# A hybrid decoder step in fp32 on one core: first branch's product between the Gated DeltaNet's steps, a hand-written TensorE order at the change of stages, residual in whole rows

## The chip, the cores and the metric

One Trainium2 chip, one core. The metric is the device time of one launch in microseconds (us). The kernel before takes 2064.81 us, the median of three runs (2064.51 to 2070.0).

## What is computed

One step of a one-layer decoder trunk on 1032 tokens (1024 of a prompt, 8 new ones of a sample), width 1024, all in fp32. Cut to what matters here (RWKV-7 gives `o_a`, the Gated DeltaNet `o_b`, both 512 wide):

```
proj = rmsnorm(h) @ w_in
o_a = rwkv7(proj);  o_b = gated_delta_chunked(conv(proj))
gate_a, gate_b = sigmoid(...)
mix = gate_a * (o_a @ w_branch_a) + gate_b * (o_b @ w_branch_b)
h = h + mix @ w_out
u2 = rmsnorm(h)
h = h + (silu(u2 @ w_ffn_gate) * (u2 @ w_ffn_up)) @ w_ffn_down
h = h + sigmoid(rmsnorm(h) @ w_ple_gate) * (pe @ w_ple_proj);  y = rmsnorm(h)
# gated_delta_chunked: tinv = (I + L)^-1 for each chunk and head, then
v_new = u_c - w_c @ S;  o = qg_c @ S + qk_c @ v_new
S = S * gl_c + kd_c.T @ v_new            # eight chunks (0 to 7), in turn
```

## The kernel before

Tokens lie along the free axis, channels on the 128 partitions: 1032 columns in 3 blocks of 344, or 4 of 258. Each fp32 product is three TensorE products (`mm`, L75), high half by high, high by low, low by high, which add up in a PSUM tile named `acc`. `weights` loads a tile of weights `ws` on SyncE's queue (SP), ScalarE (ACT) copies the high half `wh` (L186), GpSimd (POOL) subtracts for the low half `wl` (L187). `split` does the same with data on ACT and VectorE (DVE) (L246, L247).

The first half runs under `order` (L112). A stream of the 46 tiles of the input product is cut into single `acc` products, and tasks (RWKV features, chains of small products, the DeltaNet's inverses, steps, preparations, posts) come back when a clock of `mm`'s making has moved on: `yield 64.0` means "after 64 us of products". So TensorE's order is fixed when the program is built. `inverses` (L1065) inverts 32 x 32 triangles on DVE, ends that part with three transposes to AN and tm (L1090 to L1092), yields 64.0, then issues thin 32 x 32 products (`f<-AN,LT`, `f<-tm,LT`, `f<-LT,W`) four at a time between stream products, has GpSimd clear the tile W (L1128), and issues 64 x 64 products. GpSimd also carries a chain of updates for the sample's state (`St`, `st`, L1190 to L1198).

`steps`, `preps` and `posts` are the DeltaNet's chunks: a step is `x<-S,kc`, `o<-S,q`, `x<-X,LT`, `x<-x,Kd`, `o<-x,M` in turn, a post transposes (`f<-cs,ob`) and normalises to `ob_d` in DRAM. When the tasks are done, `o_a` and `o_b` are loaded in whole rows to U and split, then branch a is a plain `dense` (L1388 to L1390: 288 products of 344 columns, evacuated by DVE into U), then branch b (384 of 258), whose evacuation is a gate load, DVE (L1416), GpSimd's add of U (L1417) and a split to `mx`.

From there a priority scheduler sets the order. `mixer_out(t)` for the two halves t of the tokens adds the input x, stores the residual to `h_d`, and gathers squares; `square` then sends the sum through a product with ones (`f<-c`), `inv_rms` (DVE, with `f<-nre`) and an ACT copy to R. `mixes(t)` multiplies by the norm (L1452) and makes the Strassen operands `xh`, `xl` (L1461 to L1464). The per-layer product `ph` (144 products of 344 columns) follows `mixer_out(1)`; then come the FFN's gate and up products in Strassen form (the first gate product does half t=0 before t=1) and, per group of hidden tiles, the down product, which loads and stores the residual in blocks (L1619, L1626).

Of the kernel before, what the change touches and what calls it, by code (L numbers as in the profile page):

```python
# [9 lines left out]
F32 = mybir.dt.float32  # L10
# [16 lines left out]
KT = 8  # L27
# [31 lines left out]
def hybrid(ctx, tc, a, o):  # L59
# [102 lines left out]
    def scratch(name, shape):  # L162
        return o[name] if name in o else dram.tile(shape, F32, name=name)
# [38 lines left out]
    def cols(b):  # L202
        return b if isinstance(b, slice) else slice(b * BW, (b + 1) * BW)
# [83 lines left out]
    def stream(jobs):  # L287
# [45 lines left out]
        for n, ti in enumerate(jobs[3:], 3):  # L333
            if n == 3:
                nxt = fetch(ti)
            w = nxt
            tc.cur_priority -= LATER
            if n + 1 < len(jobs):
                nxt = fetch(jobs[n + 1])
            tc.cur_priority += LATER  # L340
            for b in range(NBLK):
                yield from product(ti, *w, b)

    def kvr(f):
        return [4 + f, 8 + f, f]
# [720 lines left out]
    def inverses():  # L1066
# [78 lines left out]
    def gdn_sample():  # L1145
# [207 lines left out]
    tasks += [Task(-2 * LATER, steps()), Task(U_, preps()), Task(-LATER, posts())]  # L1353
    order(tasks, dense_in, list(tasks))
    gstk.close()
    psg.close()


    ustk, astk, bstk = ExitStack(), ExitStack(), ExitStack()
    hU = pool(ustk, "hU", 1, "right")  # L1360
    U = [hU.tile([P, TOK], F32, name=f"U{m}") for m in range(KT)]

    def pair(pl_, name, n):
        return [[pl_.tile([P, TOK], F32R, name=f"{name}{q}{k}") for k in range(n)] for q in "hl"]

    obh, obl = pair(pool(bstk, "brb", 1, "right"), "ob", HB)
    oah, oal = pair(pool(astk, "bra", 1, "right"), "oa", 4)
    for src, hi, lo, u0 in ((oa_d, oah, oal, 0), (ob_d, obh, obl, 4)):
        for f in range(4):
            SP.dma_start(U[u0 + f], src[f])  # L1370
        for b in range(NBLK):
            for f in range(4):
                split(U[u0 + f][:, cols(b)], None, hi[f][:, cols(b)], lo[f][:, cols(b)])
    order([], dense_in, [])
    xstk.close()
    tstk = ExitStack()
    tmp = pool(tstk, "tmp", 2)
    banks += 2 * [ctx.enter_context(tc.tile_pool(name="psn", bufs=4, space=PSUM))]

    depth = [3]  # L1380

    def tile(tag, n=BW):
        return tmp.tile([P, n], F32, tag=tag, name=tag, bufs=depth[0] if tag == "a" else 2)

    for m in range(KT):
        def evac(b, ps, m=m):
            g = tile("a")
            SP.dma_start(g, gate_d[m, :, cols(b)])  # L1388
            stt(U[m][:, cols(b)], g, 1.0, ps, ADD, MULT)
        dense(a["wa"][m], 4, oah, oal, evac)  # L1390
    astk.close()
    QW, HW = TOK // 4, TOK // 2
    QB = [slice(i * QW, i * QW + QW) for i in range(4)]
    pas, m1stk, m0stk, xastk, pbs, sstk = (ExitStack() for _ in range(6))
    hq = [pool(pas, "h0", 1), None]
    H, RN, mx = [None, None], [None, None], [None, None]

    def part_of_h(t):
        H[t] = [hq[t].tile([P, HW], F32, name=f"H{t}{m}") for m in range(KT)]
        RN[t] = hq[t].tile([P, HW], F32, name=f"R{t}")  # L1400

    part_of_h(0)
    mx[1], mx[0] = pool(m1stk, "mx1", 1), pool(m0stk, "mx0", 1)
# [6 lines left out]

    for m in range(KT):
        def evac(c, ps, m=m):
            g = tile("a")[:, :QW]
            SP.dma_start(g, gate_d[KT + m, :, c])
            y = tile("c")[:, :QW]
# [3 lines left out]
        dense(a["wb"][m], HB, obh, obl, evac, QB)  # L1419
    bstk.close()  # L1420
    ustk.close()

    def square(m, c, src, ac, R, pl_, newd, last=False):

        if m == 0:
            act(ac, src, AF.Square)
            return
        d = newd(width(c))
        act(d, src, AF.Square)
        if m < KT - 1:  # L1430
            gtt(ac, ac, d, ADD)
            return
        ps = ft([P, width(c)])
        if last:
            mm(ps, ones, ac, start=True, stop=False)
        else:
            tt(d, d, ac, ADD)
        mm(ps, ones, d, start=not last, stop=True)
        inv_rms(R, ps, pl_, ft)
# [5 lines left out]
    def mixes(pl_, t):  # L1445


        hi, lo = ([pl_.tile([P, 4, QW], F32R, tag=f"x{q}{i}", name=f"x{q}{t}{i}") for i in range(7)] for q in "hl")
        tc.cur_priority += (2 - t) * LATER
        y = []  # L1450
        for m in range(KT):
            stt(H[t][m], H[t][m], vc("nffn", m), RN[t], MULT, MULT)  # L1452
            y.append([H[t][m][:, :QW], H[t][m][:, QW:]])
        for i in SIX:
            for k in range(4):
                (y11, y12), (y21, y22) = y[k], y[k + 4]
# [8 lines left out]
        tc.cur_priority -= (2 - t) * LATER  # L1465
        return hi, lo

    def mixer_out(t):
        sq = [hq[t].tile([P, QW], F32, tag=f"sq{i}", name="sq") for i in range(2)]
        for m in range(KT):  # L1470
            def evac(c, ps, m=m):
                i = c.start // QW % 2
                x = tile("a")[:, :QW]
# [15 lines left out]
    for k in range(2):
        for b in range(NBLK):  # L1490
            y = tile("a")
            SP.dma_start(y, a["peT"][k, :, cols(b)])
            split(y, None, ph[k][:, cols(b)], pl[k][:, cols(b)])
    mixer_out(1)
    m1stk.close()
    pas.close()
    tstk.close()
    hstk = ExitStack()
    xb = pool(ctx, "xm1", 1)
    XM[1] = mixes(xb, 1)  # L1500
    sgp = pool(hstk, "sg", 1)
    for m in range(KT):
        po = sgp.tile([P, TOK], F32, tag=f"sg{m % 2}", name="po")

        def evac(b, ps, m=m, po=po):
            act(po[:, cols(b)], ps, AF.Copy)
            SP.dma_start(pp_d[m, :, cols(b)], po[:, cols(b)])
        dense(a["wpp"][m], 2, ph, pl, evac)
    sg = [sgp.tile([P, TOK], F32, tag=f"sg{i}", name=f"sg{i}") for i in range(2)]

    def strassen(src, j, evac, apart=False):
# [64 lines left out]
        for x in second:  # L1578
            part(*x)

    f0 = 0
    for n in (2, 4, 4, 4, 4, 4):
        for j in range(0, n, 2):
# [11 lines left out]
            if f0 + j == 0:  # L1595
                pbs.close()
                hp = pool(hstk, "hid")
                hh, hl = pair(hp, "hid", 4)
                tmp = pool(hstk, "tf", 2)
                depth[0] = 6  # L1600
            strassen(a["wu"], f0 + j, up)
        final = f0 + n == NF
        if final:
# [9 lines left out]
            R = ux.tile([P, TOK], F32, name="R")  # L1613
            idr = diagonal(ux, EW)
        for m in range(KT):
            def evac(b, ps, m=m):
                c = cols(b)
# [119 lines left out]
```

## Time and profile before

| | us |
|---|---|
| median of the runs | 2064.81 |
| the profiled execution | 2082.16 |
| its span | 2080.3 |
| TensorE busy | 1953.9 (94%) |
| DVE busy | 1326.4 (64%) |
| ACT busy | 847.1 (41%) |
| GpSimd busy | 995.5 (48%) |
| mean granted clock of TensorE | 0.962 of full |

Busy shares are means over stages with different limits. A clock column of 1.00 is 2.4 GHz, 0.50 is 1.2 GHz. An idle time in brackets behind an instruction is its engine's wait, with what ended it.

### The profile page before, as it was taken

How to read it: one execution, taken by the hardware profiler on the slowest of the kernel's cores; microseconds unless marked ns; L12 is line 12 of the kernel's file. 1: busy time of each engine (PE TensorE's matmuls, PEld its weight loads, DVE VectorE, ACT ScalarE, POOL GpSimd, SP SyncE). 2: the span in 40 equal slices, each digit the busy share in tenths (PEclk: the TensorE clock that was granted, in tenths of full speed). 3: DMA queues.
4: the chain of work that ended last, by engine and by line, in shares of the span. 5: the costliest groups of instructions: out<-in, count | busy, mean ns of one | idle time of the engine just before them, and what ended most of it. 6: DMA issues, size and time to landing. Idle time of an engine off the chain costs nothing.

```text
span 2080.3 us, 40640 instructions
## 1 busy us (share of the span) xinstructions
PE 1953.9 (94%) x14904; PEld 1826.7 (88%) x14904; DVE 1326.4 (64%) x3300; ACT 847.1 (41%) x2069; POOL 995.5 (48%) x1084
## 2 busy tenths in 40 slices
PE   7988999898999999999799988799999999999996
PEld 7987788776788879899799978799999999999995
DVE  7378676897998369536553787464643635446767
ACT  3333354555554342147423454241423414235532
POOL 1455453666573246641056553553645546364722
PEclk9998999999999999689899999999999999999998
DMA  4442332342343436444446542625244262433312
GB/s 149 142 131 77 109 106 69 111 133 81 93 136 112 147 90 172 143 123 134 166 138 178 159 148 80 188 62 174 77 123 138 72 187 69 135 110 114 109 49 92
DMA packets 218496, 250.89 MB, mean 121 GB/s; under 512 B 48408, under 2 KB 176296, under 8 KB 218296
## 3 DMA queue, kind: packets, MB, share of 16 engines
q1 hardware_dynamic: 218296, 248.30, 39.3%
q8 instruction: 117, 1.92, 0.4%
q14 instruction: 83, 0.68, 0.1%
HBM read 170.82 MB, written 77.40 MB: 119 GB/s over the span
## 4 chain that ended last, share of the span: by engine, by line
PE 55%; DVE 14%; issue 4%; ACT 3%; DMA 2%; POOL 1%; SPq 0%; DVEq 0%; ACTq 0%; POOLq 0%
PE acc L75 48%; PE f L75 2%; PE c L75 1%; DVE xl L1464 1%; PE f L79 1%; PE x L75 1%; DVE ms L1461 1%; DVE inv L731 1%; DVE H L1452 1%; PE zp L75 1%; ACT uxh L249 1%; DVE tm L1085 1%; DVE GM L694 1%; DVE U L1620 0%; PE o L75 0%
## 5 line engine op out<-in xcount | busy, mean ns | idle before, releaser
L75 PE MATMUL acc<-xh,wh 128*128 128x258 f32 (+2 forms) x2360 | 734.1, 312 | 17.5 <-ACT wh L186 8.8
L75 PE MATMUL acc<-xl,wh 128*128 128x258 f32 (+2 forms) x2360 | 737.2, 313 | 13.5 <-DVE xl L1464 7.0
L75 PE MATMUL acc<-xh,wl 128*128 128x258 f32 (+1 forms) x2336 | 726.8, 312 | 0.0
L187 POOL TENSOR_TENSOR wl<-ws,wh 128x512 fp32r<-128x512 f32 (+1 forms) x256 | 336.1, 1315 | 455.9 <-ACT wh L186 452.5
L75 PEld LDWEIGHTS acc<-xh,wh 128*128 128x128 f32 (+1 forms) x2360 | 454.6, 193 | 25.5 <-ACT wh L186 9.0
L75 PEld LDWEIGHTS acc<-xl,wh 128*128 128x128 f32 (+1 forms) x2360 | 456.2, 193 | 23.4 <-DVE xl L1464 8.2
L75 PEld LDWEIGHTS acc<-xh,wl 128*128 128x128 f32 x2336 | 451.6, 193 | 5.5
L186 ACT ACTIVATE wh<-ws 128x512 fp32r<-128x512 f32 (+1 forms) x256 | 157.2, 615 | 254.2 <-PE acc L75 202.6
L187 POOL TENSOR_TENSOR wl<-s,wh 128x512 fp32r<-128x512 f32 x110 | 143.5, 1306 | 148.9 <-ACT wh L186 143.5
L75 PE MATMUL acc<-hidl,wh 128*128 128x344 f32 x528 | 169.4, 321 | 0.0
L75 PE MATMUL acc<-hidh,wh 128*128 128x344 f32 x528 | 166.9, 320 | 2.6 <-DVE a L1620 1.9
L75 PE MATMUL acc<-hidh,wl 128*128 128x344 f32 x528 | 168.8, 320 | 0.0
L1620 DVE TENSOR_TENSOR a<-a,acc 128x344 f32<-128x344 f32 x120 | 60.9, 512 | 125.5 <-PE acc L75 108.7
L186 ACT ACTIVATE wh<-s 128x512 fp32r<-128x512 f32 x110 | 69.3, 631 | 150.1 <-PE acc L75 103.9
L1570 POOL TENSOR_TENSOR s<-ws 128x512 f32<-128x512 f32 x66 | 87.7, 1330 | 53.0 <-DMA ws<-in_wg 44.6
L75 PEld LDWEIGHTS acc<-hidh,wh 128*128 128x128 f32 x528 | 98.8, 188 | 4.1 <-DVE a L1620 1.6
L75 PEld LDWEIGHTS acc<-hidl,wh 128*128 128x128 f32 x528 | 99.3, 188 | 0.3 <-DVE hidl L247 0.3
L75 PEld LDWEIGHTS acc<-hidh,wl 128*128 128x128 f32 x528 | 99.3, 188 | 0.0
L454 POOL TENSOR_TENSOR cy<-cy,cu 128x344 f32<-128x344 f32 x72 | 70.4, 978 | 48.8 <-ACT cu L453 47.4
L75 PE MATMUL acc<-mxh,wh 128*128 128x258 f32 x256 | 72.7, 284 | 0.0
L75 PE MATMUL acc<-mxl,wh 128*128 128x258 f32 x256 | 72.6, 284 | 0.0
L75 PE MATMUL acc<-mxh,wl 128*128 128x258 f32 x256 | 72.2, 282 | 0.0
(469 smaller groups left out, 4018.8 us busy)
## 6 DMA issues: line engine op xcount, KB each, us to landing
ws<-in_win SPq DMA_DIRECT2D x92, 256.0 KB, 3.3
a<-h_d SPq DMA_DIRECT2D x120, 172.0 KB, 2.7
h_d<-a SPq DMA_DIRECT2D x120, 172.0 KB, 2.7
pa_d<-gs SPq DMA_DIRECT2D x90, 172.0 KB, 2.3
ws<-in_wg SPq DMA_DIRECT2D x44, 256.0 KB, 3.2
ws<-in_wu SPq DMA_DIRECT2D x44, 256.0 KB, 3.0
ws<-in_wd SPq DMA_DIRECT2D x40, 256.0 KB, 2.7
gate_d<-gs SPq DMA_DIRECT2D x48, 172.0 KB, 2.5
```

The costliest lines, as they stand in the source:

```text
L75: last[0] = TE.matmul(out, w, x, start=start, stop=stop).ins
L79: last[0] = TE.transpose(out, x, ident).ins
L186: act(h, s, AF.Copy)
L187: (eng or gtt)(l, s, h.bitcast(F32), SUB)
L249: act(hi, src, AF.Copy, scale=gain)
L454: gtt(y, y, u, ADD)
L694: stt(GM[:, 2 * (c + j) + h], ps[h][:, j], cvf[:, cg, h:h + 1], rwmask, MULT, MULT)
L731: tt(w, XA[:, :ns, :nj], LB[:, i:i + 1, :nj].to_broadcast([P, ns, nj]), MULT)
L1085: tt(tm4[:, :i, :i], XT4[:, :i, :i], LB4[:, i:i + 1, :i].to_broadcast([P, i, i]), MULT)
L1452: stt(H[t][m], H[t][m], vc("nffn", m), RN[t], MULT, MULT)
L1570: e(s, A_[p], A_[q], op)
L1620: tt(y, y, ps, ADD)
```

## The change

1. `inverses` yields 68.0 in place of 64.0.
2. Branch a becomes a task, `branch_a`, whose products are taken between the DeltaNet's steps; it loads `o_a` in blocks into the input tiles `xh`, `xl` (0 to 3), and its results go to a new DRAM tensor `u_d`. `branch_b` loads and splits `o_b` as the posts 2, 5 and 7 end. U and its whole-row loads go; branch b's evacuation loads `u_d`.
3. From `mixer_out(0)` to the per-layer product TensorE's order is as written. The sums of squares of a half go in one `sums_of_squares` (one ones-product per quarter, one `rsq` for both), the norm stays in PSUM, and L1452's 8 multiplications of 516 columns become 16 of 258.
4. The down product's residual moves in whole rows of 1032 columns.

```diff
-        yield 64.0
+        yield 68.0
...
+    def branch(src, f, b, k):
+        y = gsp.tile([P, BW], F32, tag="cy", name="ab")
+        SP.dma_start(y, src[f, :, cols(b)])
+        split(y, None, xh[k][:, cols(b)], xl[k][:, cols(b)])
+    def branch_a():
+        yield "win", "branches"
...
+        nxt = weights(a["wa"][0], 4)
+        yield 6.0
+        for m in range(KT):
+            wh, wl = nxt
+            for b in range(NBLK):
...
+                SP.dma_start(g, gate_d[m, :, c])
...
+                    yield 0.0
+                stt(g, g, 1.0, ps, ADD, MULT)
+                SP.dma_start(u_d[m, :, c], g)
...
+    def branch_b():
+        for b, m in enumerate((2, 5, 7)):
+            yield "win", ("post", m), "sampled"
+            for h in range(HB):
+                branch(ob_d, h, b, 4 + h)
...
-            g = tile("a")[:, :QW]
+            g, u = tile("a"), tile("u")
             SP.dma_start(g, gate_d[KT + m, :, c])
+            SP.dma_start(u, u_d[m, :, c])
...
-            gtt(y, y, U[m][:, c], ADD)
+            gtt(y, y, u, ADD)
...
+        for g in range(2):
+            ps = ft([P, QW])
+            mm(ps, ones, sq[g], start=True, stop=True)
+            tt(e[:, g], ps, idr, MULT)
...
-            stt(H[t][m], H[t][m], vc("nffn", m), RN[t], MULT, MULT)
+            for g in range(2):
+                stt(y[m][g], R[g], vc("nffn", m), y[m][g], MULT, MULT)
...
+    with tc.manual_schedule(engines={mybir.EngineType.PE}):
...
+        mixer_out(1, (0,), sq1)
+        e = sums_of_squares(0, sq)
+        mixer_out(1, (1,), sq1)
+        XM[0] = mixes(xa, 0, e)
...
+        for m in range(KT):
+            per_layer(m)
+            if m == 1:
+                e = sums_of_squares(1, sq1)
+            if m == 3:
+                XM[1] = mixes(xb, 1, e)
...
-                y = U[m][:, c] if final else tile("a")
-                SP.dma_start(y, h_d[m, :, c])
+            y = U[m] if final else rows.tile([P, TOK], F32, tag="row", name="row")
+            SP.dma_start(y, h_d[m])
...
+            if not final:
+                SP.dma_start(h_d[m], y)
```

The tile pool of `u` holds two buffers, that of `row` three.

TensorE at the end of the DeltaNet's steps, before: the last stream products, then two steps with nothing between, the last posts, and branch a.

```order
L75 MATMUL x<-x,Kd 128x128 x4
L75 MATMUL o<-x,M 128x128 x4
L79 MATMUL f<-cs,v 128x128 x4
L75 MATMUL f<-q,kc 128x128 x4
L75 MATMUL x<-S,kc 128x128 x4
L75 MATMUL o<-S,q 128x128 x4
L79 MATMUL f<-cs,q 128x128 x4
L75 MATMUL x<-X,LT 128x128 x4
L75 MATMUL x<-x,Kd 128x128 x4
L75 MATMUL o<-x,M 128x128 x4
L79 MATMUL f<-cs,ob 128x128 x8
L75 MATMUL acc<-oah_11765,wh 128x344 x3
```

The same place with the change: branch a's products stand in the last step (`xh_102` to `xh_105` are the input tiles that now hold `o_a`).

```order
L75 MATMUL x<-X,LT 128x128 x2
L75 MATMUL acc<-xh_104,wh 128x344
L75 MATMUL acc<-xl_112,wh 128x344
L75 MATMUL acc<-xh_104,wl 128x344
L75 MATMUL acc<-xh_105,wh 128x344
L75 MATMUL acc<-xl_113,wh 128x344
L75 MATMUL acc<-xh_105,wl 128x344
L75 MATMUL x<-x,Kd 128x128 x4
L75 MATMUL o<-x,M 128x128 x4
```

What moved: 3 to 9 products of branch a lie between the small ones of the last steps, and one step stays without.

DVE behind `mixer_out(1)`, before: the sum of the first Strassen operands (`s<-ws`, of two weight tiles) near the end of the first of two norm chains.

```order
L241 SCALAR_TENSOR_TENSOR nrr<-nrr 128x3
L242 SCALAR_TENSOR_TENSOR nrr<-nrr 128x3
L240 TENSOR_TENSOR nrr<-nrr 128x3
L241 SCALAR_TENSOR_TENSOR nrr<-nrr 128x3
L1570 TENSOR_TENSOR s<-ws 128x512
L242 SCALAR_TENSOR_TENSOR nrr<-nrr 128x3
L282 TENSOR_SCALAR nre<-idr,nrr 128x128 x2
L282 TENSOR_SCALAR nre<-idr,nrr 128x2
L273 TENSOR_TENSOR nre<-f,idr 128x258
```

The same place with the change.

```order
L1501 TENSOR_TENSOR sq_13744<-sq_13744,c 128x258
L1612 TENSOR_TENSOR s<-ws 128x512
L1452 TENSOR_TENSOR e_14621<-f,idr_14541 128x258 x2
L1453 TENSOR_REDUCE r_14620<-e_14621 128x2
L1454 TENSOR_REDUCE r_14620<-e_14621 128x1
```

What moved: `s<-ws` stands ahead of the one chain that is left. On TensorE the ones-product of t=1 came behind 15 `ph` products; with the change the two stand behind 36, and the two products `f<-e` 36 behind those.

SP at the first down product, before: the next gate's last weights behind the residual's blocks (all 24 loads and 21 of 24 stores stand ahead).

```order
L1626 DMA h_d<-a 128x344
L1619 DMA a<-h_d 128x344
L1626 DMA h_d<-a 128x344
L1520 DMA ws<-in_wg 128x512
L1626 DMA h_d<-a 128x344 x2
L1520 DMA ws<-in_wu 128x512
L1626 DMA h_d<-a 128x344
```

The same with the change: the weights go ahead of most rows.

```order
L1562 DMA ws<-in_wg 128x512
L1691 DMA h_d<-row 128x1032
L1562 DMA ws<-in_wg 128x512
L1691 DMA h_d<-row 128x1032
L1562 DMA ws<-in_wu 128x512
L1679 DMA row<-h_d 128x1032
```

What moved: the fourth load of `in_wg` stands behind three loaded rows and one stored row, and no longer behind 24 loads and 21 stores.

## Rows read from the trace of the kernel before

**Rows 1.** The page, busy time of each engine
```profile
PE 1953.9 (94%) x14904; PEld 1826.7 (88%) x14904; DVE 1326.4 (64%) x3300; ACT 847.1 (41%) x2069; POOL 995.5 (48%) x1084
```

**Rows 2.** Busy time by stretch (us, then busy and count of each engine, clock, DMA)
```profile
852.00:894.00 42.00, 42.00 (x386) 32.88 (x386) 9.77 (x28) 8.52 (x15) 28.71 (x39) 0.50 0.49 142
...
962.00:988.00 26.00, 23.49 (x191) 22.91 (x190) 17.48 (x68) 22.08 (x93) 3.21 (x5) 1.00 0.49 137
988.00:1012.00 24.00, 13.01 (x89) 10.71 (x90) 12.74 (x50) 11.78 (x51) 0.00 (x0) 0.79 0.34 104
1012.00:1016.00 4.00, 4.00 (x16) 4.00 (x17) 4.00 (x10) 3.91 (x11) 0.00 (x0) 0.58 1.02 417
...
1060.00:1105.00 45.00, 45.00 (x379) 45.00 (x377) 30.60 (x61) 16.48 (x38) 32.98 (x38) 1.00 0.48 135
...
1345.00:1800.00 455.00, 455.00 (x3496) 455.00 (x3495) 238.21 (x479) 162.06 (x345) 228.87 (x177) 1.00 0.37 113
```

**Rows 3.** Timeline of PE where the thin products begin
```profile
849.12 0.32 PE L75 MATMUL acc<-xl,wh 128*128 128x344 f32 x1
849.37 0.24 PE L75 MATMUL f<-AN,LT 32*32 32x32 f32 x2
851.28 0.21 PE L75 MATMUL f<-tm,LT 32*32 32x32 f32 x1 [1.67 <-DVE tm L1092]
```

**Rows 4.** Timeline of POOL in the thin stretch
```profile
873.57 0.61 POOL L1195 TENSOR_TENSOR st<-kr,sw 128x256 f32<-128x256 f32 x1 [0.67 <-DVE sw L1194]
...
878.16 0.61 POOL L1195 TENSOR_TENSOR st<-kr,sw 128x256 f32<-128x256 f32 x1 [0.99 <-DVE sw L1194]
...
892.11 1.80 POOL L1128 MEMSET W<- 64x2048 f32 x1 [0.83 <-PE f L75]
```

**Rows 5.** PE's waits, 975 to 1016 (total, times, longest), and tile U's splits (ns)
```profile
PE f L79 <- ACT ob L1342: 6.4, 3, 2.9
PE acc L75 <- ACT oah L246: 6.0, 1, 6.0
...
L246 ACT ACTIVATE oah<-U x12: 473/475/497, 1011.3 to 1015.9; 128x344 fp32r<-128x344 f32 x12
```

**Rows 6.** Groups of branch b's evacuation, 1062 to 1104 (busy, mean ns)
```profile
L1417 POOL TENSOR_TENSOR c<-c,U 128x258 f32<-128x258 f32 x29 | 21.7, 749 | 11.1 <-DVE c L1416 8.4 <-ACT wh L186 2.3
...
L1416 DVE SCALAR_TENSOR_TENSOR c<-a,acc 128x258 f32<-128x258 f32 x29 | 12.3, 424 | 6.1 <-PE acc L75 4.2
```

**Rows 7.** DMA issues: branch b, whole span, 990 to 1020 (KB, us to landing)
```profile
a<-gate_d SPq DMA_DIRECT2D x29, 129.0 KB, 2.2
...
a<-h_d SPq DMA_DIRECT2D x120, 172.0 KB, 2.7
...
U<-oa_d SPq DMA_DIRECT2D x4, 516.0 KB, 5.3
```

**Rows 8.** Timeline of DVE from the end of `mixer_out(1)`
```profile
1217.74 0.69 DVE L1570 TENSOR_TENSOR s<-ws 128x512 f32<-128x512 f32 x1 [2.77 <-DMA ws<-in_wg]
...
1221.50 0.43 DVE L273 TENSOR_TENSOR nre<-f,idr 128x258 f32<-128x258 f32 x1 [1.23 <-PE f L75]
...
1230.38 9.59 DVE L1452 SCALAR_TENSOR_TENSOR H<-H,vec,R 128x516 f32<-128x516 f32 x8 [1.87 <-ACT R L285]
...
1271.28 0.42 DVE L1464 TENSOR_TENSOR xl<-ms,xh 128x258 fp32r<-128x258 f32 x1
```

**Rows 9.** PE's products of tile `ph`, and the wait in them on its timeline
```profile
L75 PE MATMUL acc<-ph,wh x48: 317/320/850, 1200.3 to 1233.1; 128*128 128x344 f32 x48
...
1209.68 1.23 PE L75 MATMUL f<-c,cs 128*128 128x258 f32 x2 [6.82 <-DVE c L1437]
```

**Rows 10.** PE's and POOL's waits around the first down product
```profile
PE acc L75 <- ACT wh L186: 8.8, 1, 8.8
...
POOL s L1570 <- DMA ws<-in_wg: 25.8, 1, 25.8
```

**Rows 11.** Busy time of the stretch there
```profile
1319.00:1330.00 11.00, 4.55 (x23) 4.56 (x24) 4.51 (x6) 2.19 (x4) 5.79 (x5) 0.53 0.85 261
```

More of the change, by code (lines that the diff above doesn't have):

```diff
@@ L178, in hybrid @@
     h_d = scratch("h_d", [8, P, TOK])
+    u_d = scratch("u_d", [8, P, TOK])
     wst = pool(ctx, "wst", 3)
@@ L342, in stream @@
                 yield from product(ti, *w, b)
+        mark("win")
     def kvr(f):
@@ L1351, in post @@
         SP.dma_start(ob_d[:, :, m * P:m * P + P].rearrange("h p t -> p h t"), zs)
-    tasks += [Task(-2 * LATER, steps()), Task(U_, preps()), Task(-LATER, posts())]
+    def branch(src, f, b, k):
[5 more added lines that the diff above has]
+        for b in range(NBLK):
+            for f in range(4):
+                branch(oa_d, f, b, f)
+        nxt = weights(a["wa"][0], 4)
+        yield 6.0
+        for m in range(KT):
+            wh, wl = nxt
+            for b in range(NBLK):
+                c = cols(b)
+                g = gsp.tile([P, BW], F32, tag="gs", name="gs", bufs=3)
+                SP.dma_start(g, gate_d[m, :, c])
+                ps = psd.tile([P, BW], F32, tag="acc", name="acc")
+                for k in range(4):
+                    mm(ps, wh[k], xh[k][:, c], start=(k == 0), stop=False)
+                    mm(ps, wh[k], xl[k][:, c], start=False, stop=False)
+                    mm(ps, wl[k], xh[k][:, c], start=False, stop=(k == 3))
+                    yield 0.0
+                stt(g, g, 1.0, ps, ADD, MULT)
+                SP.dma_start(u_d[m, :, c], g)
+                if b == 0 and m + 1 < KT:
+                    nxt = weights(a["wa"][m + 1], 4)
@@ L1354, in hybrid @@
+    def branch_b():
[3 more added lines that the diff above has]
+                branch(ob_d, h, b, 4 + h)
+    tasks += [Task(-2 * LATER, steps()), Task(U_, preps()), Task(-LATER, posts()), Task(3 * U_, branch_b()),
+              Task(4 * U_, branch_a())]
     order(tasks, dense_in, list(tasks))
+    order([], dense_in, [])
     gstk.close()
     psg.close()
-    ustk, astk, bstk = ExitStack(), ExitStack(), ExitStack()
@@ L1360, in hybrid @@
[L1360 to L1373, printed above, removed]
@@ L1374, in hybrid @@
-    order([], dense_in, [])
     xstk.close()
+    QW, HW = TOK // 4, TOK // 2
+    QB = [slice(i * QW, i * QW + QW) for i in range(4)]
     tstk = ExitStack()
@@ L1378, in hybrid, with tile @@
     banks += 2 * [ctx.enter_context(tc.tile_pool(name="psn", bufs=4, space=PSUM))]
[L1380 to L1393, printed above, removed]
+    def tile(tag, n=QW):
+        return tmp.tile([P, n], F32, tag=tag, name=tag, bufs=4 if tag == "a" else 2)
     pas, m1stk, m0stk, xastk, pbs, sstk = (ExitStack() for _ in range(6))
     hq = [pool(pas, "h0", 1), None]
[L1396 removed]
+    H, mx = [None, None], [None, None]
     def part_of_h(t):
         H[t] = [hq[t].tile([P, HW], F32, name=f"H{t}{m}") for m in range(KT)]
[L1400 removed]
     part_of_h(0)
@@ L1412, in evac @@
         def evac(c, ps, m=m):
-            g = tile("a")[:, :QW]
+            g, u = tile("a"), tile("u")
             SP.dma_start(g, gate_d[KT + m, :, c])
-            y = tile("c")[:, :QW]
+            SP.dma_start(u, u_d[m, :, c])
+            y = tile("c")
             stt(y, g, 1.0, ps, ADD, MULT)
-            gtt(y, y, U[m][:, c], ADD)
+            gtt(y, y, u, ADD)
             split(y, None, of(mh, m, c), of(ml, m, c))
[L1419 to L1439, printed above, removed]
+        dense(a["wb"][m], HB, xh[4:8], xl[4:8], evac, QB)
+    xpstk.close()
     sp, sx = pool(sstk, "sp", 2, "right"), pool(sstk, "sx", 1, "right")
@@ L1466, in mixes, with mixer_out @@
         return hi, lo
-    def mixer_out(t):
-        sq = [hq[t].tile([P, QW], F32, tag=f"sq{i}", name="sq") for i in range(2)]
-        for m in range(KT):
+    def mixer_out(t, ms, sq):
+        for m in ms:
             def evac(c, ps, m=m):
                 i = c.start // QW % 2
-                x = tile("a")[:, :QW]
+                x = tile("a")
                 SP.dma_start(x, a["xT"][m, :, c])
@@ L1489, in hybrid @@
[L1489 to L1497, printed above, removed]
-    hstk = ExitStack()
[L1499 to L1508, printed above, removed]
@@ L1509, in hybrid, with squares @@
-    sg = [sgp.tile([P, TOK], F32, tag=f"sg{i}", name=f"sg{i}") for i in range(2)]
+                if m == 0:
+                    act(sq[i], h, AF.Square)
+                    return
+                d = tile("c")
+                act(d, h, AF.Square)
+                (gtt if m < KT - 1 else tt)(sq[i], sq[i], d, ADD)
+            dense(a["wo"][m], KT, mh[t], ml[t], evac, QB[2 * t:2 * t + 2], HW * t)
+    def squares(t):
+        return [hq[t].tile([P, QW], F32, name=f"sq{t}{i}") for i in range(2)]
@@ new lines, in hybrid, with per_layer, evac @@
+    hstk = ExitStack()
+    with tc.manual_schedule(engines={mybir.EngineType.PE}):
+        sq = squares(0)
+        mixer_out(0, range(KT), sq)
+        m0stk.close()
+        XM = [None, None]
+        xa = pool(xastk, "xm0", 1, "right")
+        hq[1] = pool(pbs, "h1", 1, "right")
+        part_of_h(1)
+        ph, pl = ([hq[1].tile([P, TOK], F32R, name=f"p{q}{k}") for k in range(2)] for q in "hl")
+        sq1 = squares(1)
+        mixer_out(1, (0,), sq1)
+        e = sums_of_squares(0, sq)
+        mixer_out(1, (1,), sq1)
+        XM[0] = mixes(xa, 0, e)
+        for k in range(2):
+            for c in QB:
+                y = tile("a")
+                SP.dma_start(y, a["peT"][k, :, c])
+                split(y, None, ph[k][:, c], pl[k][:, c])
+        mixer_out(1, range(2, KT), sq1)
+        e1 = hq[1].tile([P, QW], F32, name="idr1")
+        G.tensor_copy(e1, idr)
+        idr = e1
+        m1stk.close()
+        pas.close()
+        tstk.close()
+        xb = pool(ctx, "xm1", 1)
+        sgp = pool(hstk, "sg", 1)
+        def per_layer(m):
+            po = sgp.tile([P, TOK], F32, tag=f"sg{m % 2}", name="po")
+            def evac(b, ps):
+                act(po[:, cols(b)], ps, AF.Copy)
+                SP.dma_start(pp_d[m, :, cols(b)], po[:, cols(b)])
+            dense(a["wpp"][m], 2, ph, pl, evac)
+        for m in range(KT):
[4 more added lines that the diff above has]
+                XM[1] = mixes(xb, 1, e)
+        sg = [sgp.tile([P, TOK], F32, tag=f"sg{i}", name=f"sg{i}") for i in range(2)]
@@ L1579, in strassen, with pair, square @@
             part(*x)
+    def pair(pl_, name, n):
+        return [[pl_.tile([P, TOK], F32R, name=f"{name}{q}{k}") for k in range(n)] for q in "hl"]
+    def square(m, c, src, ac, R, pl_, newd, last=False):
+        if m == 0:
+            act(ac, src, AF.Square)
+            return
+        d = newd(width(c))
+        act(d, src, AF.Square)
+        if m < KT - 1:
+            gtt(ac, ac, d, ADD)
+            return
+        ps = ft([P, width(c)])
+        if last:
+            mm(ps, ones, ac, start=True, stop=False)
+        else:
+            tt(d, d, ac, ADD)
+        mm(ps, ones, d, start=not last, stop=True)
+        inv_rms(R, ps, pl_, ft)
     f0 = 0
```

44 lines of the change are left out of this document (24 added, 20 removed).

## Prediction

> **What bounds the kernel now.** I read the page first: TensorE is busy 94% of the span, every other engine far less [rows 1]. What a change can win is thus TensorE's idle time, some 126 us (2080.3 less 1953.9), and the time it works at half clock. The busy times by stretch tell where these lie: in the long FFN part TensorE is busy 455 of 455 us at clock 1.00, so nothing that lies beside it there costs anything; the thin stretch is busy 42 of 42 us but at clock 0.50; the end of the DeltaNet's steps is half idle [rows 2]. The timelines and waits [rows 3 to 5, 8 to 10] name who is late in each. I set the sum against the profiled execution, 2082.16 us, which is 17 us (0.8%) above the median of the runs, 2064.81, and subtract the same amount from the median. TensorE's products of 258 columns come every 45.0 / 379 = 0.119 us at full clock [rows 2]; those of 344 then take 0.119 x 344 / 258 = 0.158.
>
> **Part 1, yield 68.0.** The first thin products start at 849.37, and the next wait 1.67 us for DVE's last transpose, until 851.28 [rows 3]. The added 4.0 us of products are 27 stream products by the built order, 27 x 0.158 = 4.3 us, more than 1.67: the wait goes. Behind that wait the clock falls to 0.50, and stays there for the 42 us of the stretch [rows 2], though TensorE is never idle in it. If nothing drops the clock, the work of 42 us at half takes 21. But it can't all be kept. The 64 x 64 products behind need the tile W that GpSimd clears, and GpSimd's order is fixed: with the change the clear comes behind one more sample step. Steps began at 873.57 and 878.16, 4.6 us apart [rows 4]; the next would begin near 883, its three operations (0.6 to 0.7 each) and a weight's low half bring the clear to about 887, and with its 1.8 us [rows 4] to 889. Before, it ended at 892.11 + 1.80 = 893.9. So TensorE stands still from about 875 to 889, and resumes 5 us earlier than before, with 27 products (4.3 us) more done: **-9 us**. Bounds: -2 if the thin stretch runs at half clock all the same (only the wait is saved), -21 if GpSimd is not late.
>
> **Part 2, branch a between the steps.** From 962 to 1016 TensorE is idle 2.51 + 10.99 = 13.5 us, and loses 1.7 us to the clock from 1012 to 1016 (4 x 0.42) [rows 2]. The named waits are 6.4 us for posts on ACT and 6.0 us for the splits of the loaded `o_a` [rows 5]. With branch a's 3 to 9 products (0.5 to 1.4 us) between small products these waits have cover; the 288 products cost the same wherever they stand. One step stays without cover, for which I leave one of the three post waits, about 2.5 us. 13.5 + 1.7 - 2.5: **-13 us**. What could take it back is ACT: it is busy 22.08 of 26 us there, and 24 splits come in, 12 of each branch, of 0.475 us each [rows 2, 5], 11.4 us; where all of it falls into such a stretch it overflows by 7.5, so -5.5; if the last uncovered step costs nothing, -17. VectorE's 24 evacuations are only moved. The 24 stores of `u_d` and the loads in front go through SP, whose queue has no weights with a near use behind them; TensorE takes branch a's weights one tile ahead.
>
> **Branch b's evacuation.** It adds 32 loads of 129 KB. The nearest row is the gate's load of the same size, 2.2 us to landing [rows 7]. Tile `u` has two buffers; each is held for a load and until GpSimd's addition, 0.75 us [rows 6], ends: (2.2 + 0.75) / 2 = 1.48 us per block, where TensorE takes 12 x 0.1187 = 1.42. That is 0.06 x 32 = 2 us late, and with the issue of the next load some more: **+3 us**, between 0 (PSUM hides it) and +8 (0.25 us per block).
>
> **Part 3, the change of stages.** `ph` begins at 1200.3 and TensorE waits 6.82 us in it [rows 9], but the true pace is VectorE's: its multiplications by the norm start at 1230.38 and the last Strassen operand is out at 1271.28 [rows 8], 41 us later; TensorE needs that operand for its last gate products. With the change the ones-products of t=1 stand behind 36 `ph` products, at 1200.3 + 36 x 0.158 = 1206. But VectorE's queue then has `s<-ws` first, which before waited 2.77 us for its weights, until 1217.74 [rows 8]. Those weights stand on SP behind `ph`'s own, whose buffers come free as TensorE takes `ph`; without the 6.82 us wait I put them that much earlier, 1211. One norm chain took from 1221.50 to 1230.38, 8.9 us, including a 0.69 us sum and a copy by ACT [rows 8]; without these I take 7. So the multiplications start at 1211 + 0.7 + 7 = 1219, take 16 x 0.424 = 6.8 instead of 9.6 us (the price of an operation that reads 258 columns from PSUM [rows 6]), and the last operand is out at 1219 + 41 - 2.8 = 1257: **-14 us**. Bounds: -7 if `s<-ws` is as late as before; -20 if the weights are there in time and the chain starts at 1206.
>
> **Part 4, whole rows.** In the first down product TensorE waits 8.8 us for weights whose load GpSimd waited 25.8 us for [rows 10], because SP has them behind the residual's blocks in the order. Behind that wait 4.55 us of work ran at clock 0.53 [rows 11], which is 2.2 us. Now the loads go ahead of most rows: **-11 us**, at least -3.5 if the first row's load takes 5.3 us as one of 516 KB did [rows 7] and puts off the store ahead of the weights. In the other groups everything lies under TensorE's 455 of 455 us [rows 2]: 0, the price without that cover being 8 x (5.3 - 2.7) = 21 us per group [rows 7].
>
> **Sum.** -9 - 13 + 3 - 14 - 11 = -44: 2038 us for the profiled execution, 2021 for the median.
>
> **Rivals.**
> *The thin products stay at half clock* (0.25). For: the clock stays at 0.50 for 42 us with TensorE never idle [rows 2], so the thin work may not hold it up by itself. Against: it fell behind the only wait there. Part 1 is then -2 and the sum -37: 2028.
> *VectorE's and ACT's queues give part of it back* (0.12): `s<-ws` holds the norm chain to 1217.74 (-7 instead of -14), and ACT's splits the steps (-5.5 instead of -13). Sum -29.5: 2035.
> *The first rows come late* (0.03): a block of 172 KB lands in 2.7 us, a row of 516 KB in up to 5.3 [rows 7]; if every group's first evacuation waits for that, TensorE loses 6 x 2.6 = 16 us. Against: TensorE waits for no residual in 455 of 455 us [rows 2]. Sum -28: 2037. A rule points this way: the Trainium skill, Perfetto Trace Analysis, section DMA Optimizations, says that splitting transfers into smaller chunks may let some start sooner; no wait in these rows bears it out here.
> *The two buffers of `u` set the pace, and it is slower* (0.06). TensorE can't leave branch b before the last block. The gain of 44 us is eaten when each of 32 blocks takes 1.42 + 44 / 32 = 2.8 us, which is when a load takes 2 x 2.8 - 0.75 = 4.8 us. At the 5.3 us of the whole-row loads [rows 7] a block takes 3.0, branch b 51 us more, the kernel 2072. For: the loads read what was stored shortly before, through the same queue in order. Against: loads of this size and place land in 2.2.
> *The waits only move* (0.04): what is won before 1060 runs into the same late weights, what is won at the change of stages into VectorE; within 6 us of 2065.
>
> **How the numbers follow.** The forecast as summed has 0.5. The likeliest is 2021; the sum of all good ends is -72, of all bad ones -10, which would hardly fall together. Leaving out a tenth on each side, -22 to -68 remain: 1997 to 2043. A measurement tells 0.3% (6 us) from no change. All cases but the last two are faster by more: 0.90; same 0.04; slower 0.06.
>
> **What would show it.** In the profile after: no wait behind `f<-AN,LT` and clock 1.00 in the thin stretch, with a wait of some 10 us for GpSimd's clear of W; busy over 0.9 in the last steps; branch b's products in 45 us or a little more, with waits (if any) that lead to `u`; the norm's multiplications of t=1 starting near 1219 less what was won ahead of it, with a short wait of TensorE at `f<-e`; no wait for `wh` in the first down product. It would be wrong if the thin stretch is still at 0.50, if `mixer_out(0)` waits for `mx`, or if the FFN groups show waits for `row`.

## The result: slower by 0.9%

The changed kernel takes 2086.96 us (median of five runs, 2081.89 to 2091.25) against 2065.6 of the kernel before; the ratio is 1.009, with a 95% interval of 1.0063 to 1.0117. The prediction said 2021 and faster. The profiled execution took 2087.77 us, against 2082.16 before.

TensorE's products of three tiles mark the stages (mxh belongs to `mixer_out`, hid to the first down product, uxh to the products behind the FFN). Each row has the first and the last start; before, mxh went from 1104.8 to 1200.0, hid began at 1290.2 and uxh at 1957.5. After:

```profile
L75 PE MATMUL acc<-mxh,wh x256: 277/283/777, 1110.9 to 1220.3; 128*128 128x258 f32 x128
...
L75 PE MATMUL acc<-hidh,wh x528: 315/319/426, 1304.8 to 1961.0; 128*128 128x344 f32 x176
...
L75 PE MATMUL acc<-uxh,wh x192: 279/336/578, 1961.5 to 2062.6; 128*128 128x384 f32 x128, 128*128 128x264 f32 x64
```

| stage (us, profiled executions) | before | after | forecast of the difference |
|---|---|---|---|
| to the last product with W (908.5, 897.0) | 908.5 | 897.0 | -9 |
| from there to `mixer_out` | 196.3 | 213.9 | -10 (parts of -13 and +3) |
| `mixer_out` to `ph` | 95.5 | 109.7 | 0 |
| `ph` to the first hid product | 89.9 | 84.2 | -14 |
| from there to the first uxh product | 667.3 | 656.7 | -11 |

In this pair the first and the last row went as forecast, and the second and third gave all of it back. The pair is one execution of each. Their spans differ by 5.7 us only, because the one of before was 17 us above its median; and three kernels below that are as before in `mixer_out` (`b_again`, `b_y68`, `b_rows`) took 97 to 100 us for it in place of 95.5. The busy times by stretch of after (columns as in [rows 2]) show it: the thin stretch at 0.92 in place of 0.50, but the DeltaNet's last steps (950 to 1023) and what was branch a and b (1023 to 1111) idle in every piece, where before 1060 to 1105 had been 45.00 of 45.00.

```profile
852.00:894.00 42.00, 37.82 (x513) 31.05 (x512) 12.67 (x35) 11.63 (x21) 34.21 (x46) 0.92 0.63 174
...
950.00:985.00 35.00, 27.55 (x168) 24.40 (x165) 22.36 (x72) 23.31 (x86) 2.60 (x2) 0.85 0.59 172
985.00:1023.00 38.00, 34.49 (x229) 32.33 (x230) 22.47 (x74) 19.90 (x76) 3.87 (x3) 0.91 0.47 144
1023.00:1060.00 37.00, 32.49 (x204) 31.15 (x203) 9.28 (x18) 4.99 (x9) 5.97 (x5) 0.96 0.62 188
1060.00:1111.00 51.00, 43.64 (x333) 40.98 (x332) 27.33 (x54) 15.53 (x34) 30.12 (x37) 0.99 0.68 193
1111.00:1166.00 55.00, 49.73 (x386) 49.23 (x387) 13.72 (x28) 18.51 (x38) 33.37 (x34) 0.94 0.62 183
```

The waits name the new ones (total, times, longest), first from 897 to 1060, then from 1060 to 1221 (with GpSimd's for `u`), then from 1221 to 1305:

```profile
PE acc L75 <- ACT xh L247: 8.0, 5, 3.1
...
PE acc L75 <- DVE gs L1383: 3.4, 2, 2.2
...
PE x L75 <- ACT x L1315: 3.2, 4, 2.4
...
POOL c L1435 <- DMA u<-u_d: 19.7, 15, 2.8
...
PE acc L75 <- DVE c L1434: 7.3, 10, 2.3
...
PE f L75 <- DVE e L1458: 4.9, 2, 4.7
PE acc L75 <- ACT mxh L247: 4.9, 1, 4.9
...
PE f L75 <- DVE e L1458: 7.6, 1, 7.6
...
PE acc L75 <- DVE xl L1483: 4.6, 4, 1.4
```

`xh` are the splits of the loaded `o_a`, `gs` is branch a's gate tile, `c` and `mxh` are branch b's evacuation, `e` is the norm chain. The posts' waits of [rows 5], 6.4 us, are down to 0.4; others came.

Why TensorE waits for `c`: GpSimd's addition, which frees `c`, waits for the loads of `u`, and SP's timeline shows these in pairs, as many as there are buffers. The pair of 1077.26 and that of 1106.06 are eight pairs apart: 28.8 us for 16 blocks, 1.80 us per block, where TensorE takes 1.42.

```profile
1077.26 1.34 SPq L1432 DMA_DIRECT2D u<-u_d  x2
...
1106.06 1.02 SPq L1432 DMA_DIRECT2D u<-u_d  x2
```

And the loads of `o_a`, through two tiles, come six in 9.8 us (start and duration of the row); all twelve are issued between 963.97 and 989.08, 25 us:

```profile
966.58 9.78 SPq L1360 DMA_DIRECT2D ab<-oa_d  x6
```

Meanwhile SP waits for stores to `u_d` to land (950 to 1060), because the next gate is loaded into the tile that they leave:

```profile
SPq L1376 <- DMA u_d<-gs: 28.5, 15, 3.5
```

VectorE after `mixer_out(1)`: the sum `s<-ws` waits 5.73 us for its weights, with the norm chain behind it.

```profile
1226.82 0.75 DVE L1501 TENSOR_TENSOR sq<-sq,c 128x258 f32<-128x258 f32 x1 [2.46 <-ACT c L1500]
...
1233.30 0.69 DVE L1612 TENSOR_TENSOR s<-ws 128x512 f32<-128x512 f32 x1 [5.73 <-DMA ws<-in_wg]
1233.91 0.75 DVE L1452 TENSOR_TENSOR e<-f,idr 128x258 f32<-128x258 f32 x2
...
1240.95 1.14 DVE L1458 TENSOR_SCALAR e<-idr,r 128x128 f32<-128x128 f32 x6
1242.89 6.39 DVE L1472 SCALAR_TENSOR_TENSOR H<-f,vec,H 128x258 f32<-128x258 f32 x16 [0.80 <-PE f L75]
...
1283.96 0.41 DVE L1483 TENSOR_TENSOR xl<-ms,xh 128x258 fp32r<-128x258 f32 x1
```

### The profile page after: what moved, and what is told of

Same layout as the page of the kernel before. It is cut to its first block, busy times and chain, and to the rows that moved or that the text cites. A ratio compares the mean times of both kernels' runs of the same rounds, so it can differ in the third digit from the quotient of the medians.

```text
span 2086.0 us, 40354 instructions
## 1 busy us (share of the span) xinstructions
PE 1951.4 (94%) x14904; PEld 1822.1 (87%) x14904; DVE 1317.5 (63%) x3294; ACT 847.5 (41%) x2067; POOL 997.4 (48%) x1085
## 5 line engine op out<-in xcount | busy, mean ns | idle before, releaser
L75 PE MATMUL acc<-xh,wh 128*128 128x258 f32 (+2 forms) x2584 | 799.3, 310 | 27.8 <-ACT xh L247 8.0
L75 PE MATMUL acc<-xl,wh 128*128 128x258 f32 (+2 forms) x2584 | 799.0, 310 | 12.2 <-DVE xl L251 6.9
L75 PE MATMUL acc<-xh,wl 128*128 128x258 f32 (+1 forms) x2560 | 789.6, 309 | 0.0
L75 PEld LDWEIGHTS acc<-xh,wh 128*128 128x128 f32 (+1 forms) x2584 | 492.7, 191 | 40.2 <-ACT xh L247 9.6
L75 PEld LDWEIGHTS acc<-xl,wh 128*128 128x128 f32 (+1 forms) x2584 | 493.6, 191 | 23.7 <-DVE xl L251 8.5
L75 PEld LDWEIGHTS acc<-xh,wl 128*128 128x128 f32 x2560 | 491.1, 192 | 5.3
L1683 DVE TENSOR_TENSOR row<-row,acc 128x344 f32<-128x344 f32 x120 | 60.4, 512 | 125.3 <-PE acc L75 114.8
```

The costliest lines, as they stand in the source:

```text
L75: last[0] = TE.matmul(out, w, x, start=start, stop=stop).ins
```

## The experiments

Ratios are against the kernel before, run beside them on the same chip, with their 95% intervals. Its median beside them was 2067.2 us (`b_again` to `a_u4`), 2069.6 (`a_ab5` to `b_stage`), 2070.7 (`nobr_s` to `ab5_blk`) and 2069.5 (`ab5_s_blk`), so medians of different groups compare to some 3 or 4 us only.

**The kernel before again, and part 1 alone.** The trace of before gave 9 to 11 us to part 1; the first question was whether the median holds that, too. `b_again` is before unchanged, `b_y68` has one edit:

```diff
-        yield 64.0
+        yield 68.0
```

> The kernel before, unchanged, profiled again. Its first profiled execution took 2082.16 us and its five other runs 2064.5 to 2073.4. Theory A (the thin stretch runs at half clock only in some executions): a profiled execution near 2065, with the thin stretch (852 to 894) at clock 1.00 and its 42 us shortened by about 17. Rival B (the profile itself costs 17 us): again near 2082, with the thin stretch at 0.50.

> Part 1 alone: yield 68.0 on the kernel before. Theory A (most executions of before already hold full clock there): within 0.3% of before, 2062 to 2068. Rival B (part 1 gains in every execution what the two profiles show, 10 us): about 2055.

Measured: `b_again` 2069.18 us (2063.59 to 2079.56; ratio 0.9987, 0.9963 to 1.0011), its profiled execution 2073.26; `b_y68` 2071.86 us, ratio 1.0007 (0.9988 to 1.0026). So part 1 alone is worth nothing that can be measured, and rival B of the second falls (the 2072 lies above the 2062 to 2068 of theory A, the ratio within its 0.3%). The profiled execution of `b_again` lies between the two theories of the first, 9 us below the earlier one. Its thin stretch:

```profile
852.00:894.00 42.00, 42.00 (x378) 34.05 (x378) 7.43 (x22) 8.98 (x16) 26.23 (x35) 0.58 0.47 134
```

That is mostly half clock again, where theory A had 1.00; but two kernels below whose program is the same as before's up to there, `b_stage` and `b_rows`, had in their profiled executions:

```profile
852.00:894.00 42.00, 40.34 (x469) 32.34 (x467) 13.16 (x33) 10.79 (x20) 32.44 (x43) 0.76 0.53 158
```

```profile
852.00:894.00 42.00, 36.95 (x482) 30.70 (x476) 10.47 (x32) 10.76 (x19) 30.98 (x43) 0.92 0.56 165
```

The same instructions, behind a wait for `tm` of 1.4 to 1.7 us, ran at 0.50, 0.58, 0.76 and 0.92. The window is fixed in time and the work begins at different times in it, so the work itself has to be measured, from the first thin product (the first start of `f<-AN,LT`) to the last product with W (the last start of `f<-LT,W`). In `b_again`, then in `b_rows`:

```profile
L75 PE MATMUL f<-AN,LT x128: 191/222/296, 842.5 to 897.1; 32*32 32x32 f32 x64, 128*64 128x64 f32 x64
...
L75 PE MATMUL f<-LT,W x192: 222/236/270, 856.5 to 900.2; 32*32 32x32 f32 x128, 128*64 128x64 f32 x64
...
L75 PE MATMUL f<-AN,LT x128: 191/217/369, 847.9 to 893.9; 32*32 32x32 f32 x64, 128*64 128x64 f32 x64
...
L75 PE MATMUL f<-LT,W x192: 191/191/368, 857.7 to 897.0; 32*32 32x32 f32 x128, 128*64 128x64 f32 x64
```

| profiled execution | clock, 852 to 894 | first thin product | last with W | between |
|---|---|---|---|---|
| before | 0.50 | 849.4 | 908.5 | 59.1 |
| `b_again` | 0.58 | 842.5 | 900.2 | 57.7 |
| `b_stage` | 0.76 | 851.8 | 901.2 | 49.4 |
| `b_rows` | 0.92 | 847.9 | 897.0 | 49.1 |
| `b_y68` (68.0) | 0.92 | 853.6 | 899.6 | 46.0 |

Two things follow. The half clock costs 8 to 10 us where it lasts, and of the 9 us between before and `b_again` 7 had come ahead of the first thin product, so it is not what sets them apart. And `b_y68`, with the 4.3 us of products moved ahead added, took 50.3 us, no less than the two executions of before's program at the higher clock: in `b_y68` and `b_rows` TensorE waits 4.4 and 5.0 us for GpSimd's W. With 68.0 the ten profiled executions of this study all show 0.92 to 0.96 from 852 to 894. How often before has it is not known: four executions were seen.

**Without part 2, and with four buffers of u.** `a_nobr` is the change with branch a and b as before (parts 1, 3 and 4). `a_u4` is the change with

```diff
-bufs=4 if tag == "a" else 2)
+bufs=4 if tag in "au" else 2)
```

> The change without part 2 (parts 1, 3 and 4; branch a and b as before). Theory A (part 2 costs all of the loss: 17 us from the end of the thin products to the start of mixer_out, and the wait for mx behind it): faster than before, about 2065 - 10 (first down product) - 2 = 2053. Rival B (the order at the change of stages loses as much, mixer_out took 109.7 us against 95.5): 2065 or more.

> The change with four buffers for tile u in place of two. Theory A (two buffers set the pace of branch b, 1.8 us per block against 1.42): TensorE's waits for VectorE's c in branch b (7.3 us) and for mxh in mixer_out (4.9 us) go, with 3 us of low clock: about 2087 - 14 = 2073. Rival B (the loads come late because SP issues them in order behind others, not for want of a buffer): 2085 or more, with the waits still there.

Measured: `a_nobr` 2057.97 us, ratio 0.9922 (0.9897 to 0.9946); `a_u4` 2074.09 us, ratio 1.0009 (0.9991 to 1.0028). So the other three parts together make the kernel 0.8% faster, and part 2 costs 1.009 - 0.9922 = 1.7%, some 35 us, or 2086.96 - 2057.97 = 29 us by the medians. Of these two buffers of 1 KB per partition are nearly half: 2086.96 - 2074.09 = 13 us by the medians, 0.8% by the ratios, as theory A expected within about 1 us. TensorE's waits in `a_u4`, from 902 to 1109 (where `c` was 7.3 us) and from 1109 to 1212 (where mxh was 4.9):

```profile
PE acc L75 <- ACT xh L247: 9.6, 6, 3.2
PE x L75 <- ACT x L1315: 3.2, 4, 2.3
PE acc L75 <- DVE gs L1383: 2.9, 2, 2.2
PE acc L75 <- DVE c L1434: 1.8, 2, 1.4
...
PE f L75 <- DVE e L1458: 4.4, 1, 4.4
PE acc L75 <- ACT mxh L247: 1.1, 1, 1.1
```

**The tiles of the loads and of the gate.** Both take tiles of the same pool that are idle by then, so the pool doesn't grow: `a_ab5` for the loads, `a_ab3g5` three for the loads and five for the gate. Both have four u buffers. `spare` goes round the tags in its list.

```diff
-        y = gsp.tile([P, BW], F32, tag="cy", name="ab")
+        y = spare(0, ['cy', 'cr', 'cu', 'cy', 'cr'])
```

```diff
-        y = gsp.tile([P, BW], F32, tag="cy", name="ab")
+        y = spare(0, ['cy', 'cu', 'cy'])
...
-                g = gsp.tile([P, BW], F32, tag="gs", name="gs", bufs=3)
+                g = spare(1, ['gs', 'gs', 'gs', 'cr', 'cr'])
```

> The change with four u buffers, and the loads of o_a and o_b for the splits in turn into five idle tiles of the same pool (tags cy, cr, cu) in place of two. With four u buffers alone it took 2074. Theory A (the two load buffers make the splits late, TensorE's waits for xh of 7 to 8 us in the last steps, each followed by low clock): waits for xh under 2 us, about 2074 - 10 = 2064. Rival B (the loads stand in SP's queue behind stores and gate loads that wait, so more buffers help little): 2070 to 2074, waits for xh moved, not gone. Rival C (the cost is the switching between stream and small products): 2074, with the waits gone.

> The change with four u buffers, three tiles in turn for the loads of o_a and o_b, and five in place of three for branch a's gate tile, which holds the load, the product's result and its store. Theory A (the gate tile is held until its store to u_d has landed, SP waits 28.5 us for that and everything in its queue waits with it): TensorE's waits for gs (3 us) gone and those for xh smaller, about 2066. Rival B (only the load buffers matter): 2072 or more, waits for gs unchanged.

Measured: 2062.12 us (0.9943, 0.9916 to 0.997) and 2062.33 us (0.9955, 0.9933 to 0.9977). Either edit gives 11 to 14 us. Waits of `a_ab5`, 897 to 1094, then of `a_ab3g5`, 898 to 1095, and in the last two rows SP's in `a_ab3g5`, 950 to 1055:

```profile
PE x L75 <- ACT x L1315: 4.0, 5, 2.0
PE acc L75 <- DVE gs L1391: 3.9, 3, 2.5
PE acc L75 <- DVE c L1442: 3.1, 2, 2.8
...
PE acc L75 <- ACT xh L247: 0.9, 1, 0.9
...
PE acc L75 <- ACT xh L247: 3.5, 5, 1.2
...
PE acc L75 <- DVE cr L1391: 1.2, 1, 1.2
PE acc L75 <- DVE gs L1391: 0.5, 1, 0.5
...
SPq L1384 <- DMA u_d<-gs: 15.4, 10, 3.1
SPq L1384 <- DMA u_d<-cr: 13.0, 6, 4.2
```

So theory A of `a_ab5` holds: of the 9.6 us for xh 0.9 are left, and the twelve loads of `o_a`, issued over 26 us in `a_u4`, are issued over 14. Theory A of `a_ab3g5` holds in part: xh is down to 3.5 and the gate tile's wait from 2.9 to 1.7, but SP still waits 15.4 + 13.0 = 28.4 us for stores to `u_d` to land, and 25.3 in `a_ab5`. That wait by itself is therefore not what the 11 to 14 us were; what shrank in both is the time over which the loads of `o_a` come (16.5 us in `a_ab3g5`). How much of `a_ab3g5` is its third load tile and how much its gate tiles can't be told, since it has both. The part still isn't ahead of `a_nobr`.

**Parts 4 and 3 alone.** `b_rows` is before with the diff of part 4, `b_stage` with that of part 3.

> Part 4 alone on the kernel before. Theory A (part 4 is worth what the first down product loses, 8.8 us and 2.2 us of low clock, and nothing elsewhere): 2067 - 11 = 2056, TensorE's time from the first hid product to the first uxh product down from 666 to 657. Rival B (the gain is taken back elsewhere, rows late in other groups): 2062 or more.

> Part 3 alone on the kernel before. Theory A (it moves the waits: fewer for xl, new ones for e in mixer_out and in the per-layer product): within 0.3% of before, 2061 to 2073, mixer_out to the first hid product about as long as before (187 us). Rival B (what the prediction said): about 2053.

Measured: `b_rows` 2061.13 us, ratio 0.995 (0.9922 to 0.9978), theory A: 10 us by the ratio, 8.5 by the medians of that group; its hid products to uxh took 658 us in place of 666 in `b_again`. Around the first down product only one wait is left in it (1290 to 1345), and it is a new one, for the first whole row:

```profile
PE acc L75 <- DVE row L1620: 2.7, 2, 2.3
```

`b_stage` took 2067.68 us, ratio 0.9977 (0.9953 to 1.0001): theory A, with at most some 10 us and perhaps none. From `mixer_out` to the first hid product it took 186.6 us, `b_again` 187.1.

**The sum ahead of the norm chain.** In both kernels the sum for the third of the first gate's seven Strassen products, the one that stands ahead of the norm chain, goes to GpSimd: `nobr_s` is `a_nobr`, `ab5_s` is `a_ab5` with it.

```diff
-(gtt, None, tt, None, gtt, tt, gtt)):
+(gtt, None, gtt if apart else tt, None, gtt, tt, gtt)):
```

> Parts 1, 3 and 4 (as a_nobr, 2058), with the third sum of the first gate's weights on GpSimd in place of VectorE, so that s<-ws no longer stands ahead of the norm chain of t=1. Theory A (that sum's 5.8 us wait for its weights holds the chain and is what became of part 3's gain): the chain starts some 6 us earlier, TensorE's wait at f<-e (5.6 us) goes down to 1 or 2, the norm's multiplications start near 1208 in place of 1215, about 2058 - 6 = 2052. Rival B (VectorE's work, not its start, is what counts, or GpSimd then holds up the weights): 2056 to 2060.

> The whole change with four u buffers, five load tiles and that sum on GpSimd. Theory A: 2062 - 6 = 2056. Rival B: 2060 to 2064.

Measured: `nobr_s` 2052.7 us, ratio 0.9902 (0.9864 to 0.9939); `ab5_s` 2051.3 us, ratio 0.9911 (0.9882 to 0.9941). The intervals overlap those without the edit (0.9897 to 0.9946, 0.9916 to 0.997), so the traces have to decide. From `ph` to the first hid product `a_nobr` takes 86.5 us and `nobr_s` 76.8, `a_ab5` 83.8 and `ab5_s` 72.7. TensorE's wait for `e` in that stretch, 7.0 us in `a_nobr`, is gone, and VectorE's chain in `nobr_s`, where `ph` begins at 1197.3, waits nowhere longer than 1.2 us:

```profile
1206.42 0.75 DVE L1501 TENSOR_TENSOR sq<-sq,c 128x258 f32<-128x258 f32 x1 [0.55 <-ACT c L1500]
...
1207.61 0.86 DVE L1452 TENSOR_TENSOR e<-f,idr 128x258 f32<-128x258 f32 x2 [0.44 <-PE f L75]
...
1214.17 6.39 DVE L1472 SCALAR_TENSOR_TENSOR H<-f,vec,H 128x258 f32<-128x258 f32 x16 [1.20 <-PE f L75]
...
1222.14 1.78 DVE L1612 TENSOR_TENSOR s<-ws 128x512 f32<-128x512 f32 x1
```

The multiplications start 16.9 us behind `ph`, against 24.3 in `a_nobr` (1215.31 less 1191.0) and 22.3 in the change. Theory A holds, for the mechanism by the traces; the size, 10 us of the stage, is of one execution each.

**Longer pieces of branch a, and all amendments.** `ab5_blk` is `a_ab5`, `ab5_s_blk` is `ab5_s`, with

```diff
-                    yield 0.0
+                    if k == 3:
+                        yield 0.0
```

> As a_ab5 (four u buffers, five load tiles, 2062), but branch a's products come 12 in a row (one block) between the small ones, not 3. Theory A (what part 2 still costs over a_nobr is the switching: the first product behind a small one takes 0.24 us in place of 0.16, some 30 times): about 2 us less, 2060. Rival B (the small products' partners then wait less well covered, more waits for x, ob and gs): 2064 or more.

> The whole change with the three amendments: four u buffers and five load tiles, the third sum of the first gate's weights on GpSimd, branch a's products 12 in a row. If the gains of the last two add, 2051 - 3 = 2048; if they overlap, 2051. Either way faster than the kernel before by about 1%.

Measured: `ab5_blk` 2058.64 us, ratio 0.993 (0.9907 to 0.9953); `ab5_s_blk` 2049.73 us, ratio 0.991 (0.989 to 0.993). The gain of longer pieces is inside the intervals. Theory A was not tested: by TensorE's timeline branch a's products come in 19 pieces among the small ones in `a_ab5` and in 18 in `ab5_blk`, so nearly as many switches are left. In the profile the stretch from the last product with W to `mixer_out` is 191 us in both, 196 in `a_ab5` and `ab5_s`, 194 in `a_nobr`; TensorE's waits in it sum to 8.5 us in `ab5_blk` and 13.8 in `a_ab5`, so they shrank where rival B had them grow. The best two versions beat both kernels by about 1%: the change so amended, and, as good within the intervals, parts 1, 3 and 4 without part 2 (`nobr_s`).

## Why the prediction was wrong

**Part 2, forecast -13, and +3 in branch b; measured +1.7%, 29 to 35 us.** This is the step that failed. The working counted what covers each wait of before, ACT's work, and the weights on SP, and went past the tiles that the moved work uses itself: the two for the loads of `o_a` and `o_b`, and the gate's three. "The 24 stores of `u_d` and the loads in front go through SP, whose queue has no weights with a near use behind them" named the queue and then asked only for weights. What stood behind were its own loads: those of `o_a` came over 25 us, and TensorE waited 8.0 us for their splits. With five tiles they came over 14 us, and the kernel was 12 us faster; with three, and five for the gate, as much. SP's wait for stores to land, 28.5 us, was still 25 to 28 us in both. TensorE's order was fixed, so each late split stopped all steps, and behind the waits its clock fell: 0.85, 0.91 and 0.96 where 962 to 988 had been at 1.00. The gain itself did not come even so: the waits between the last product with W and `mixer_out` sum to 15.7 us in `a_nobr`, without part 2, and still to 13.8 in `a_ab5`, for other tiles.

In branch b the mechanism was right and its size wrong. The prediction had (2.2 + 0.75) / 2 = 1.48 us per block; measured is 1.80. The load took 2.6 us, not 2.2, in a stretch with 193 GB/s in place of 135, and the pair is issued in order with gates and weights. The fourth rival named the very place, "TensorE can't leave branch b before the last block", and the signs of being wrong have that `mixer_out(0)` waits for `mx`; it asked for 2.8 us per block because it set this cost alone against all the gains. 0.38 us per block, beyond the 0.25 of the upper bound, was 12 us.

**Part 1, -9 by the trace, nothing by the median.** In the trace of after no wait is left at the thin products, their clock is 0.92, TensorE waits for GpSimd's clear of W (4.2 us, forecast about 10), and the last product with W starts 11.5 us earlier. But the forecast took one execution of before, 17 us above the median, as the kernel. The step that failed is "Behind that wait the clock falls to 0.50", taken as true of every execution: of four, two had it so for all of the stretch. Where before's program ran at the higher clock it came from the first thin product to the last with W no later than with 68.0, and in `b_rows` there too TensorE waits for the clear of W (5.0 us), which the working had seen as the next bound. That the profiled execution was slower than the three others known (2064.51 to 2070.0) was on the table; the half clock explains 8 to 10 of its 17 us. The Trainium skill, TensorE: Matmul & The Clock Gate, section HAM oscillation, describes the clock falling when TensorE waits between two bursts of products; here a wait of 1.4 to 1.7 us was followed by a fall for the whole of the stretch, for a part of it, or by none.

**Part 3, -14; measured -0.2% (0 to -0.5%).** The step that failed is "I put them that much earlier, 1211": the weights of `s<-ws` were to come 10.7 us behind the first `ph` product. They came at 12.7 in the change (1233.30 less 1220.6), with a wait of 5.73 us, although TensorE no longer waited early in `ph`. Then the chain ended at 22.3 where the forecast had 18.7, and the operands took 41.5 us where it had 38.2: the saved 2.8 us of the multiplications did not come out at the end. The last operand stands 63.8 us behind the first `ph` product; 71.4 before, 57 forecast. In part 3 alone (`b_stage`) it stands at 67.1, where `b_again` has 69.9. With the sum off VectorE the multiplications started at 16.9. The wait for `e` in `mixer_out`, 4.9 us (3.5 in `b_stage`), was not in the forecast at all: half t=0 has the same chain with 48 products of cover. Executions of before have 1.4 to 3.9 us there, for `nre`.

**Part 4, -11; measured -0.5% (-5 to -16 us), -10.6 in the trace.** Right, with its place and size: 8.8 us of wait for wh gone, 2.3 to 2.6 us for the first row come. In the other groups TensorE waits for nothing in either kernel (1345 to the first uxh product). The rule of the Trainium skill that the third rival of the prediction drew on, Perfetto Trace Analysis, section DMA Optimizations, that smaller chunks may let some start sooner, thus shows in that first row only.

Together: 9, 39 to 45, 9 and 1 make 58 to 64 us between forecast and result; measured are 66 (2087 less 2021). Two slips in the working changed nothing: its good ends sum to -69, not -72, and the rival on the buffers of `u` counts the 3 us of branch b twice (47 and 2069 in place of 44 and 2072).

What stays open: why `mixer_out` takes 103 to 106 us in the amended versions with part 2 and some 100 without (waits of 5.1 and 1.3 us in `a_ab5` against 3.5 in `a_nobr`, 2.9 of the 4 us), how often before holds full clock in the thin stretch, and where the rest of its slow profiled execution was lost.

## What to carry to other kernels

When work is moved under a fixed order, count the buffers of every tile that it brings, as (landing + use + issue) / buffers against the pace of its user, and look at what shares the queue with it; here two buffers of `u` and two tiles for loads turned the other parts' gain of 0.8% into a loss. When an engine's queue has an instruction that waits for a load, ask what critical chain stands behind it. And when the profiled execution is slower than the unprofiled median, profile the same kernel again before crediting a change with what one trace shows: here three more executions showed the half clock to be there in some of them only.

## What was not expected of the hardware

The clock over one stretch is not a property of the program: four executions with the same instructions there ran 852 to 894 at 0.50, 0.58, 0.76 and 0.92, TensorE being busy 37 to 42 of the 42 us. And in `a_u4`'s timeline the first `acc` behind `f<-cs,q` keeps the next waiting 0.24 us, the others 0.16. The same shows behind most of the 19 pieces of small products among which branch a stands; what it costs in all, some 19 x 0.08 = 1.5 us, is an estimate from these gaps, and no run tested it.

```profile
1009.00 0.60 PE L79 MATMUL f<-cs,q 128*128 128x128 f32 x4
1009.36 0.40 PE L75 MATMUL acc<-xh,wh 128*128 128x344 f32 x1
1009.60 0.32 PE L75 MATMUL acc<-xl,wh 128*128 128x344 f32 x1
1009.76 0.32 PE L75 MATMUL acc<-xh,wl 128*128 128x344 f32 x1
```
